# A hybrid attention, RG-LRU and SSD decoder step on one core: loads of rows by store and reload, slots of the background streams, and banks of the output sums

## The chip, the cores and the metric

The kernel runs on one core of one Trainium2 chip. The metric is device time in microseconds of one execution. Engines are named as the profile names them: PE (TensorE matmul), PEld (its weight loads), DVE (VectorE), ACT (ScalarE), POOL (GpSimd) and SP (SyncE, which here only issues DMAs). A "q" behind a name (SPq, ACTq) is that engine's queue of DMA issues.

## The reference, cut to what matters

Two layers work on 1024 prompt tokens and on 8 sample tokens with caches. Each layer is one combined projection, three kinds of heads beside each other, and one output projection.

```python
def mixer_layer(x, pos, att_cache, lru_conv0, lru_h0, ssd_conv0, ssd_h0, p):
    proj = jnp.einsum('bld,de->ble', x, p['w_in'])
    q, k, v, g_att, x_lru, g_lru, z_ssd, xbc, dt_raw = jnp.split(proj, SPLIT_POINTS, axis=-1)
    ...
    br_a = att * jax.nn.silu(g_att)          # 8 query heads, 2 key heads, window 128, sinks
    ...
    br_b = hl * jax.nn.silu(g_lru)           # conv of 4 taps, block gates, linear recurrence
    ...
    y, ssd_h1 = ssd_scan(xh, dt, a_head, ...)  # chunks of 128 tokens, 12 heads of 64, state 128
    y = (y + D * xh) * jax.nn.silu(z_ssd)
    y = y * lax.rsqrt(jnp.mean(jnp.square(y), -1, keepdims=True) + NORM_EPS) * p['ssd_norm_g']
    mix = jnp.concatenate([br_a, br_b, y], -1)
    out = jnp.einsum('ble,ed->bld', mix, p['w_out'])
    return layer_norm(DEEPNORM_ALPHA * x + out, p['ln_g'], p['ln_b']), states
```

In an SSD chunk `a_cs` is a running sum of `dt * a_head` over the 128 tokens. The chunk needs `exp(a_cs[i] - a_cs[j])` for all pairs of tokens, so the kernel needs each head's `a_cs` both as a column and as a row that every partition holds.

## The kernel before, in words

The work is four steps, (layer, half of the tokens), one behind the other: step 0 is layer 0 with tokens 0 to 511, step 1 layer 0 with tokens 512 to 1023 and the 8 sample tokens, steps 2 and 3 the same for layer 1. Half 0 works on 512 columns, half 1 on 520, as two chunks of 260 (`chunks`). By the trace, step 0 ends near 345 us, step 1 near 815, step 2 near 1165 and step 3 at the end.

**The foreground.** `step()` calls the projections in a written order; each makes 128 output channels. A projection is 24 matmuls for 512 columns, or 24 for each of the two chunks, because every product is taken as three (`mac3`, L295 to L297: high part by high part, high by low, low by high). Its sums stand in one of three PSUM banks of the pool `ipp` (`ip_tile()`), and an operation on ACT or DVE empties the bank: `conv` (L328), `gate_silu` (L341 on ACT, L342 on DVE) or `rope`. The fourth part of a step is `out_proj`: four groups of rows (attention, the second part of the SSD rows, LRU, the rest) by eight blocks of 128 outputs, each sum again in an `ip_tile()`, added to the residual by DVE at L1044 (L1053 after the change).

**The background.** Everything else is written as Python generators in lists by name (`att`, `ssd`, `ssd_sub`, `lru`, `norm`, `tail`). Before each 12 matmuls of 512 columns or 24 of 260, `pump()` lets each of them go on by one turn; `yield n` waits n such turns (called slots here), and `spawn(list, generator, delay)` starts one after `delay` slots, 3 if none is given. The sums of the background stand in five banks of the pool `mmp` (`mm_tile()`). `drain` runs lists to their end.

* `attention_stream`: for each of 4 query groups g and 4 blocks of 128 tokens, `block` makes scores (L874, L875), a softmax (L878 to L886), waits 3 slots, transposes the probabilities (L892) and copies them out (L895, L897), waits 2 slots, multiplies by the values (L903) and gates the result into the buffer `ga` (L905). After block 3 the group's `ga` is stored to DRAM (`mixd`, L908, issued by ACT). `ga` has two buffers (`NQ`), so the third group's gate (L342) waits for the first group's store.
* `attention_sample` (half 1): the 8 sample tokens, a chain of small operations with `yield` between the parts. Scores L965 and L966, then on DVE and ACT a softmax that ends with `pr` (L977) and `dg` (L979), `yield 2`, the matmuls L982 and L983, two copies, `yield 2`, the matmuls from L990.
* `ssd_steps`: makes `dt`, `da`, and, in half 1, stores the sample tokens' decays (`sdd`, L539, rows of single numbers) and loads them back spread over the partitions (`dcols`, L542); it stores the 48 transposed running sums (`acsd`, L563).
* `ssd_stream`: for each of 2 head groups and 4 chunks, `block` loads two tiles `acr` of decay rows (L636; 3 heads each, 192 KB, `NA` = 3 buffers) from `acsd`, transposes (L639, L648), builds decays on ACT and POOL (L655 to L662), and 3 slots later multiplies (L667, L672); `weighted` (L607) reads the result. `sample(g)` does the 8 sample tokens: it stores `bcd` (L696), loads it back as `bb` (L705, a pair of tokens at a time), loads each state `h0` (L707) and stores it (L712). `squares` and L755 make the norm's sum.
* `lru_stream`: the block gates L459 want a row move inside a tile by DMA (L430) before their last quarter.

Almost all DMAs are issued by SP, in the order in which they stand. An issue that must wait (for data just stored, or for a buffer) holds all issues behind it, weights among them: `wraw` (L242), and in half 1 `wl` (L244), the low parts of the weights that half 0 computed and stored (`low`). Two projections' weights are loaded ahead (`load_weights`).

The program is built with a scheduler that lays out each engine's instructions by its own estimate of times; the order in which the code emits them is a priority only.

Of the kernel before, what the change touches and what calls it, by code (L numbers as in the profile page):

```python
# [13 lines left out]
AF = mybir.ActivationFunctionType  # L14
# [3 lines left out]
P = 128  # L18
# [23 lines left out]
NA = 3  # L42
# [9 lines left out]
def tile_trunk(ctx, tc, outs, x_t, cache_k, cache_v, st_lru_conv, st_ssd_conv, st_ssd_h, w_in, w_dt, w_out,  # L52
# [6 lines left out]
    dma = nc.sync.dma_start  # L59
# [437 lines left out]
    def ssd_steps(st, l, half, x):  # L497
# [12 lines left out]
        def rest():  # L510
# [21 lines left out]
            if half:  # L532

                sdt = wtile([NS, 2, 12], "eda")
                V.tensor_copy(sdt[:, 0, :], dt[:NS, 48:60])
                S.activation(sdt[:, 1, :], da[:NS, 48:60], AF.Exp)
                sdd = dp.tile([2, 12, NS], F32, tag="sdd", name="sdd")
                for e in range(2):
                    dma(sdd[e].rearrange("k b -> b k"), sdt.rearrange("b q (t e) -> b (q t) e", e=2)[:, :, e])  # L539
                dcols = st["dcols"] = wtile([P, 2, 6, NS], "dcols")  # L540
                for e in range(2):
                    dma(dcols[64 * e:64 * e + 64].rearrange("p a b c -> p (a b c)"),  # L542
                        bview(sdd, e * 96, [[0, 64], [1, 96]]))
            yield 7
# [18 lines left out]
            dma(acsd, acsT)  # L563
            st["steps"] = True
# [32 lines left out]
    def ssd_stream(st, l, half, mixrows):  # L597
# [30 lines left out]
        def block(g, b):  # L628
# [6 lines left out]
            for i in range(2):  # L635
                dma(acr[i], bview(acsd, (eb + 3 * i) * P, [[0, P], [1, 3 * P]]))  # L636
            pt = mm_tile()
# [49 lines left out]
        def sample(g):  # L687
# [9 lines left out]
            yield 1  # L697
# [4 lines left out]
            for b in range(NS):  # L702
                if b % 2 == 0:
                    bb = wtile([P, 2, 2, P], "bb", 2)
                    dma(bb, bview(bcd, b * 2 * P, [[0, P], [1, 4 * P]]))  # L705
                h0, u = wtile([P, 3, P], "h0", 2), wtile([P, 3, P], "sd", ND)
                dma(h0, st_ssd_h[l, b, heads].rearrange("(t e) p n -> (e p) t n", e=2))  # L707
                for t in range(3):
                    S.activation(u[:, t, :], bb[:, b % 2, 0, :], AF.Copy, scale=dcols[:, 0, t, b:b + 1])
# [3 lines left out]
                for t in range(3):  # L713
                    V.tensor_tensor_reduce(u[:, t, :], bb[:, b % 2, 1, :], h0[:, t, :], 1.0, 0.0,  # L714
                                           op0=ALU.mult, op1=ALU.add, accum_out=ysum[:, t, b:b + 1])
# [15 lines left out]
        for g in range(2):  # L731
# [6 lines left out]
            for b in range(4):  # L738
                spawn("ssd_sub", block(g, b))
                yield 4  # L740
# [116 lines left out]
    def attention_stream(st, l, half, mixrows, mixd0):  # L857
        W = HALF + NS * half

        def block(g, b, qa, ga):  # L860
# [26 lines left out]
            yield 3  # L887
# [45 lines left out]
    def attention_sample(l, qs, kn, vT, gas, mixd0):  # L933
# [46 lines left out]
        yield 2  # L980
# [7 lines left out]
        yield 2  # L988
# [19 lines left out]
    def out_proj(l, half, mixd, load_next, first):  # L1008
# [5 lines left out]
        cur = first  # L1014
        for gi, (g, _) in enumerate(GROUPS):
# [16 lines left out]
            for part in ((slice(HALF // 2, W), slice(0, HALF // 2)) if split_c else (None,)):  # L1032
                for op in range(4):
                    w = weights((l, g, op))
                    for oo in range(2):
                        pump()
                        o = 2 * op + oo
                        for cs in ([part] if part else chunks(W)):
                            out = ip_tile()[:, :cs.stop - cs.start]
# [268 lines left out]
```

## Time and profile before

| | |
|---|---|
| time, median of 3 runs (lowest, highest) | 1651.32 us (1650.24, 1659.54) |
| the profiled execution's own time | 1659.71 us |
| its span, first to last instruction | 1658.0 us |
| mean granted clock of TensorE | 0.978 of full speed |
| PE busy | 1573.9 us, 95% |
| DVE, ACT, POOL busy | 1066.0, 965.0, 642.7 us |
| DMA traffic | 337.45 MB, mean 204 GB/s |

Durations and waits below come from that one execution, 8.4 us above the median of the runs. A wait row tells how long an engine stood idle and what ended the idleness. A timeline row has the start in us, the duration in us, engine, line, operation, output <- input, and in brackets the idle time before it with its releaser.

### The profile page before, as it was taken

What the parts mean: (1) busy time and instruction counts of PE and PEld (TensorE: products, weight loads), DVE (VectorE), ACT (ScalarE), POOL (GpSimd) and SP (SyncE); (2) the same over time, 40 slices, a digit from 0 to 9 for tenths busy, and PEclk for the clock granted to TensorE, in tenths of its full rate; (3) what the DMA queues carried; (4) which work ended last, traced back from release to release, by engine and by line L of the source; (5) the groups of instructions that cost most, each with busy time, mean ns of one, the idle gap of its engine ahead of it and who ended that gap; (6) DMA issues with size and microseconds to landing.
All of it is one profiled execution on the core that took longest, in us unless ns stands there. A gap on an engine that the chain in (4) does not pass through costs nothing.

```text
span 1658.0 us, 31019 instructions
## 1 busy us (share of the span) xinstructions
PE 1573.9 (95%) x10696; PEld 1335.0 (81%) x10696; DVE 1066.0 (64%) x2220; ACT 965.0 (58%) x2136; POOL 642.7 (39%) x858
## 2 busy tenths in 40 slices
PE   8999999999989998999998999998999999989996
PEld 6777777678979897889976777775899998978895
DVE  5567659754955756775488675687435568568634
ACT  5565557633656665784256655676346666567724
POOL 5655666553112525200155565765512134341000
PEclk9999999999999998999999999999999999999998
DMA  8654566776554756587546556578865566657865
GB/s 267 192 169 152 164 184 215 270 258 206 170 165 159 235 181 204 179 286 267 186 137 209 181 151 179 153 238 290 244 212 168 171 191 210 199 159 239 303 201 195
DMA packets 210806, 337.45 MB, mean 204 GB/s; under 512 B 24132, under 2 KB 64272, under 8 KB 210600
## 3 DMA queue, kind: packets, MB, share of 16 engines
q1 hardware_dynamic: 208344, 331.27, 62.9%
q10 hardware_dynamic: 2304, 4.20, 0.7%
q8 instruction: 84, 1.38, 0.3%
q14 instruction: 74, 0.61, 0.1%
HBM read 242.76 MB, written 92.05 MB: 202 GB/s over the span
## 4 chain that ended last, share of the span: by engine, by line
PE 62%; DVE 12%; DMA 10%; ACT 6%; issue 3%; POOL 2%; SPq 1%; DVEq 0%; ACTq 0%; POOLq 0%
PE ip L295 17%; PE ip L297 17%; PE ip L296 17%; PE mm L459 2%; PE mm L672 2%; PE mm L903 2%; PE mm L892 2%; DVE u L358 1%; DMA wl<-low 1%; DVE sd L714 1%; DMA out_dram<-h 1%; DMA wraw<-in_w_out_dram 1%; PE mm L667 1%; ACT wh L245 1%; DMA h<-in_st_ssd_h_dram 1%
## 5 line engine op out<-in xcount | busy, mean ns | idle before, releaser
L295 PE MATMUL ip<-u,wh 128*128 128x260 f32 (+3 forms) x2592 | 853.0, 329 | 30.4 <-DVE u L1044 13.0
L297 PE MATMUL ip<-u,wl 128*128 128x260 f32 (+3 forms) x2592 | 839.5, 324 | 8.6 <-DMA wl<-low 7.4
L296 PE MATMUL ip<-u,wh 128*128 128x260 f32 (+3 forms) x2592 | 835.2, 322 | 0.6 <-DVE u L226 0.6
L295 PEld LDWEIGHTS ip<-u,wh 128*128 128x128 f32 x2592 | 494.6, 191 | 93.3 <-issue 22.6
L297 PEld LDWEIGHTS ip<-u,wl 128*128 128x128 f32 x2592 | 493.6, 191 | 56.4 <-DMA wl<-low 9.4
L296 PEld LDWEIGHTS ip<-u,wh 128*128 128x128 f32 x2592 | 494.5, 191 | 38.8 <-issue 2.5
L249 POOL TENSOR_TENSOR wl<-wraw,wh 128x256 fp32r<-128x256 f32 x432 | 369.7, 880 | 253.2 <-ACT wh L247 173.2
L247 ACT ACTIVATE wh<-wraw 128x512 fp32r<-128x512 f32 x216 | 134.3, 625 | 163.7 <-PE ip L296 78.1
L245 ACT ACTIVATE wh<-wraw 128x512 fp32r<-128x512 f32 x224 | 138.8, 625 | 137.3 <-PE ip L296 100.9
L1044 DVE SCALAR_TENSOR_TENSOR u<-u,ip 128x260 f32<-128x260 f32 (+3 forms) x192 | 96.8, 509 | 136.9 <-PE ip L297 132.2
L358 DVE SCALAR_TENSOR_TENSOR u<-ev,ssd_p,u 128x512 f32<-128x512 f32 x120 | 101.1, 843 | 14.6 <-ACT u L350 12.4
L882 ACT ACTIVATE sp<-sp,mx 128x257 f32<-128x257 f32 (+1 forms) x128 | 62.4, 489 | 58.7 <-DVE mx L878 58.7
L656 POOL TENSOR_TENSOR cq<-cq,u 128x384 f32<-128x384 f32 x56 | 61.7, 1104 | 78.6 <-ACT cq L655 55.4
L226 DVE TENSOR_TENSOR u<-u 128x512 fp32r<-128x512 f32 (+1 forms) x88 | 64.7, 763 | 31.2 <-ACT u L225 31.0
L662 ACT ACTIVATE acr<-acr,acs 128x128 f32<-128x128 f32 x192 | 63.4, 390 | 30.9 <-POOL acr L659 30.8
L655 ACT ACTIVATE cq<-acr 128x384 f32<-128x384 f32 x56 | 29.1, 520 | 83.0 <-DMA acr<-acsd 82.1
L358 DVE SCALAR_TENSOR_TENSOR u<-ev,lru_p,u 128x512 f32<-128x512 f32 x72 | 63.6, 886 | 19.9 <-ACT u L350 10.7
L878 DVE CUSTOM_DVE_ANT_0 sp<-mm,amask,sp 128x256 f32<-128x256 f32 (+1 forms) x128 | 54.5, 462 | 33.2 <-PE mm L875 10.4
L342 DVE SCALAR_TENSOR_TENSOR u<-ev,ip 128x260 f32<-128x260 f32 (+1 forms) x72 | 36.4, 507 | 58.4 <-ACT ev L341 58.3
L225 ACT ACTIVATE u<-u 128x512 fp32r<-128x512 f32 (+1 forms) x88 | 52.1, 626 | 31.3 <-DMA u<-mixd 18.1
L328 ACT ACTIVATE ev<-ip 128x260 f32<-128x260 f32 (+2 forms) x132 | 58.2, 442 | 11.6 <-PE ip L297 7.7
L714 DVE CUSTOM_DVE_ANT_0 sd<-bb,h 128x128 f32<-128x128 f32 x96 | 38.0, 443 | 37.8 <-POOL h L711 35.0
(280 smaller groups left out, 2128.0 us busy)
## 6 DMA issues: line engine op xcount, KB each, us to landing
wraw<-in_w_in_dram SPq DMA_DIRECT2D x304, 256.0 KB
wl<-low SPq DMA_DIRECT2D x224, 256.0 KB
low<-wl SPq DMA_DIRECT2D x216, 256.0 KB
wraw<-in_w_out_dram SPq DMA_DIRECT2D x136, 256.0 KB
acr<-acsd SPq DMA_DIRECT2D x64, 192.0 KB
u<-mixd SPq DMA_DIRECT2D x32, 260.0 KB
u<-mixd SPq DMA_DIRECT2D x32, 256.0 KB
mixd<-u SPq DMA_DIRECT2D x24, 260.0 KB
```

The costliest lines, as they stand in the source:

```text
L226: V.tensor_tensor(dl, raw, dh.bitcast(F32), ALU.subtract)
L245: S.activation(h, raw, AF.Copy)
L247: S.activation(h, raw, AF.Copy)
L249: G.tensor_tensor(low[:, c], raw[:, c], h[:, c].bitcast(F32), ALU.subtract)
L295: PE.matmul(out, wh, xh, start=first, stop=False)
L296: PE.matmul(out, wh, xl, start=False, stop=False)
L297: PE.matmul(out, wl, xh, start=False, stop=last)
L358: V.scalar_tensor_tensor(out[:, :HALF], raw[:, t:t + HALF], prm[:, wo + t:wo + t + 1], out[:, :HALF], op0=ALU.mult, op1=ALU.add)
L656: G.tensor_tensor(cq[i], cq[i], zc[:, None, 3, cs].to_broadcast([P, 3, P]), ALU.mult)
L662: S.activation(acr[i][:, e, :], acr[i][:, e, :], AF.Exp, scale=-1.0, bias=nacs[:, eb + 3 * i + e:eb + 3 * i + e + 1])
L882: S.activation(s[:, kv, :nk + 1], s[:, kv, :nk + 1], AF.Exp, scale=-1.0, bias=mx[:, kv:kv + 1], accum_out=den[:, kv:kv + 1])
L1044: V.scalar_tensor_tensor(ro, ro, ALPHA if gi == 0 else 1.0, out, op0=ALU.mult, op1=ALU.add)
```

## The change

Eight edits, none of which changes what is computed:

* `NA`: the `acr` tiles get four buffers for three.
* In `rest()` of `ssd_steps`, the load of `dcols` is written behind the `yield 7`, its store `sdd` ahead of it; and a `yield 3` stands between the store of `acsd` and the mark `steps` that lets the SSD blocks start.
* `block` of the SSD stream waits 3 slots between its two loads of `acr` and its first transposes, and is spawned with a delay of 1 for 3.
* `sample` waits 3 slots for 1 behind its store of `bcd`; `bb` is loaded for each token (128 KB, three buffers) and no longer for each pair (256 KB, two buffers).
* The attention `block` waits 4 slots for 3 ahead of its transposes.
* `attention_sample` waits 5 slots for 2 ahead of `pd` (L982), and 3 for 2 ahead of `po` (L990).
* `out_proj` takes every third sum of the first group, and every second of the others, from the five banks of `mmp` and no longer from the three of `ipp`.

Behind the edits the lines move by 1 to 9: L542 becomes L544, L636 L638, L874 L876, L892 L894, L903 L905, L908 L910, L965 L967, L982 L984, L990 L992.

```diff
--- before.py
+++ after.py
@@ -39,7 +39,7 @@
 NU = 10
 NQ = 2
 ND = 4
-NA = 3
+NA = 4
 NC = 3
 HW = 90
 FX = 1
@@ -537,11 +537,12 @@
                 sdd = dp.tile([2, 12, NS], F32, tag="sdd", name="sdd")
                 for e in range(2):
                     dma(sdd[e].rearrange("k b -> b k"), sdt.rearrange("b q (t e) -> b (q t) e", e=2)[:, :, e])
+            yield 7
+            if half:
                 dcols = st["dcols"] = wtile([P, 2, 6, NS], "dcols")
                 for e in range(2):
                     dma(dcols[64 * e:64 * e + 64].rearrange("p a b c -> p (a b c)"),
                         bview(sdd, e * 96, [[0, 64], [1, 96]]))
-            yield 7
             pc = mm_tile()
             PE.matmul(pc[:, 0:48], tri, da[:, :48], start=True, stop=True)
             PE.matmul(pc[:, 64:112], ones, da[:, :48], start=True, stop=True)
@@ -561,6 +562,7 @@
             V.tensor_copy(acsT, pa[:48, :P])
             acsd = st["acsd"] = dp.tile([48, P], F32, tag="acsd", name="acsd")
             dma(acsd, acsT)
+            yield 3
             st["steps"] = True
 
         spawn("ssd", rest())
@@ -634,6 +636,7 @@
             acr = [wtile([P, 3, P], "acr", NA) for _ in range(2)]
             for i in range(2):
                 dma(acr[i], bview(acsd, (eb + 3 * i) * P, [[0, P], [1, 3 * P]]))
+            yield 3
             pt = mm_tile()
             for i in range(4):
                 PE.transpose(pt[:, i * P:(i + 1) * P], xb[:, i, cs], ident)
@@ -694,24 +697,23 @@
             V.tensor_copy(bcr, pt[:NS, :2 * P])
             bcd = dp.tile([NS, 2 * P], F32, tag="bcd", name="bcd")
             dma(bcd, bcr)
-            yield 1
+            yield 3
             dcols = st["dcols"][:, :, 3 * g:3 * g + 3, :]
             V.tensor_tensor(dcols[:, 0], dcols[:, 0], xb[:, 0:3, cs], ALU.mult)
             ysum = wtile([P, 3, NS], "ysum")
             heads = slice(6 * g, 6 * g + 6)
             for b in range(NS):
-                if b % 2 == 0:
-                    bb = wtile([P, 2, 2, P], "bb", 2)
-                    dma(bb, bview(bcd, b * 2 * P, [[0, P], [1, 4 * P]]))
+                bb = wtile([P, 2, P], "bb", 3)
+                dma(bb, bview(bcd, b * 2 * P, [[0, P], [1, 2 * P]]))
                 h0, u = wtile([P, 3, P], "h0", 2), wtile([P, 3, P], "sd", ND)
                 dma(h0, st_ssd_h[l, b, heads].rearrange("(t e) p n -> (e p) t n", e=2))
                 for t in range(3):
-                    S.activation(u[:, t, :], bb[:, b % 2, 0, :], AF.Copy, scale=dcols[:, 0, t, b:b + 1])
+                    S.activation(u[:, t, :], bb[:, 0, :], AF.Copy, scale=dcols[:, 0, t, b:b + 1])
                 G.tensor_tensor(h0, h0, dcols[:, 1, :, b:b + 1].to_broadcast([P, 3, P]), ALU.mult)
                 G.tensor_tensor(h0, h0, u, ALU.add)
                 dma(s_ssd_h[l, b, heads].rearrange("(t e) p n -> (e p) t n", e=2), h0)
                 for t in range(3):
-                    V.tensor_tensor_reduce(u[:, t, :], bb[:, b % 2, 1, :], h0[:, t, :], 1.0, 0.0,
+                    V.tensor_tensor_reduce(u[:, t, :], bb[:, 1, :], h0[:, t, :], 1.0, 0.0,
                                            op0=ALU.mult, op1=ALU.add, accum_out=ysum[:, t, b:b + 1])
                 yield 1
             while ("ssd", g, 7) not in st:
@@ -736,7 +738,7 @@
             if half:
                 spawn("ssd_sub", sample(g))
             for b in range(4):
-                spawn("ssd_sub", block(g, b))
+                spawn("ssd_sub", block(g, b), 1)
                 yield 4
             if half:
                 spawn("tail", final_state(g))
@@ -884,7 +886,7 @@
             V.reciprocal(den, den)
             V.tensor_scalar(s[:, 0, :nk], s[:, 0, :nk], den[:, 0:1], None, op0=ALU.mult)
             S.activation(s[:, 1, :nk], s[:, 1, :nk], AF.Copy, scale=den[:, 1:2])
-            yield 3
+            yield 4
             pp = mm_tile()
             for kv in range(2):
                 for kh in range(nkh):
@@ -977,7 +979,7 @@
         V.tensor_scalar(pr, pr, m[:, 1:2], None, op0=ALU.mult)
         dg = wtile([64, 64], "dg")
         V.tensor_scalar(dg, ident[:64, :64], pr[:, P:P + 1], None, op0=ALU.mult)
-        yield 2
+        yield 5
         pd = mm_tile()
         PE.matmul(pd[:NS, :64], bsel, dg, start=True, stop=True)
         PE.transpose(pd[:, 64:128], pr[:, :P], ident[:64, :64])
@@ -985,7 +987,7 @@
         V.tensor_copy(d8, pd[:NS, :64])
         pTs = wtile([P, 64], "pTs")
         V.tensor_copy(pTs, pd[:, 64:128])
-        yield 2
+        yield 3
         po = mm_tile()
         PE.matmul(po[:, :64], kvn[:, 1, :], d8, start=True, stop=False)
         for b in range(NS):
@@ -1012,6 +1014,13 @@
         for i in range(2):
             dma(r[i][:, :, :W], xd[l, half][512 * i:512 * i + 512, :W].rearrange("(k p) w -> p k w", p=P))
         cur = first
+        outs = [0]
+
+        def out_tile(gi):
+
+            outs[0] += 1
+            return mm_tile() if outs[0] % (3, 2)[gi > 0] == 0 else ip_tile()
+
         for gi, (g, _) in enumerate(GROUPS):
             if gi == 1 and half == 0:
 
@@ -1036,7 +1045,7 @@
                         pump()
                         o = 2 * op + oo
                         for cs in ([part] if part else chunks(W)):
-                            out = ip_tile()[:, :cs.stop - cs.start]
+                            out = out_tile(gi)[:, :cs.stop - cs.start]
                             for k in range(4):
                                 mac3(out, w.part(k, slice(oo * P, oo * P + P)), mh[:, k, cs], ml[:, k, cs],
                                      k == 0, k == 3)
```

The places where the order of the program shows what moved, row by row as it stands on an engine:

On SP in step 3, where the sample tokens' decays are stored and loaded back (`wl` and `wraw` are weights, `eda` holds the decays). Before:

```order
L244 DMA wl_14408<-low_176 128x512
L242 DMA wraw_14576<-in_w_in_dram 128x512
L539 DMA sdd_14232<-eda_14229 8x12x1 x2
L542 DMA dcols_14235<-sdd_14232 64x96 x2
L244 DMA wl_14478<-low_177 128x512
L242 DMA wraw_14582<-in_w_in_dram 128x512
```

and after:

```order
L244 DMA wl_14421<-low_176 128x512
L242 DMA wraw_14592<-in_w_in_dram 128x512
L539 DMA sdd_14248<-eda_14245 8x12x1 x2
L544 DMA dcols_14528<-sdd_14248 64x96 x2
L244 DMA wl_14491<-low_177 128x512
L242 DMA wraw_14598<-in_w_in_dram 128x512
```

The load of `dcols` stands directly behind the store in both, though the code now has seven slots between them; in step 1 two row moves of the rope (L779, L780) stand between the two, before and after alike.

On PE in step 1, the sample tokens' attention from its scores (`sT`, `prod`) to the use of `dg`. A line of "..." stands for the rest of the SSD block's part (L672, L648) and 24 matmuls of the projections (L295 to L297), the one ahead of L982 for 44 of these. Before:

```order
L965 MATMUL mm_7623<-ident_77,sT_7413 64x128
L966 MATMUL mm_7623<-ones_83,prod_6858 64x1
L667 MATMUL mm_7654<-sd_7447,q_7449 128x384
...
L639 MATMUL mm_7717<-ident_77,u_6208 128x128 x4
...
L982 MATMUL mm_7794<-dg_7637,bsel_85 8x64
L983 MATMUL mm_7794<-ident_77,spr_7630 128x64
```

and after, where each "..." holds the rest of the part ahead of it (L675, L651, a second L459 row) and 24 matmuls of the projections:

```order
L967 MATMUL mm_7613<-ident_77,sT_7377 64x128
L968 MATMUL mm_7613<-ones_83,prod_6866 64x1
...
L670 MATMUL mm_7683<-sd_7493,q_7495 128x384
...
L642 MATMUL mm_7761<-ident_77,u_6149 128x128 x4
...
L459 MATMUL mm_7837<-u_7210,gw_88 32x260 x4
...
L459 MATMUL mm_7900<-u_7210,gw_88 32x260 x4
...
L984 MATMUL mm_7952<-dg_7627,bsel_85 8x64
```

Between the scores and the matmul that reads `dg` stood an SSD block's products, 24 matmuls of a projection, the next block's transposes and 44 matmuls more; now five times 24 matmuls, the SSD products, an SSD block's transposes and two pairs of gates stand there.

On PE in step 1, in the attention blocks (`sp` is the buffer of scores and of transposed probabilities). Before, with 24 projection matmuls at the "...":

```order
L903 MATMUL mm_5904<-sp_5768,vtok_93 64x128 x4
L892 MATMUL mm_5910<-ident_77,sp_5701 128x128 x4
...
L874 MATMUL mm_5982<-kh0_89,qa_5327 128x256
L875 MATMUL mm_5982<-kl0_91,qa_5327 128x256
L874 MATMUL mm_5982<-kh1_90,qa_5328 128x256
L875 MATMUL mm_5982<-kl1_92,qa_5328 128x256
L903 MATMUL mm_6039<-sp_5915,vtok_93 64x128 x4
```

and after, the same place with nothing left out:

```order
L905 MATMUL mm_5929<-sp_5801,vtok_93 64x128 x4
L894 MATMUL mm_5935<-ident_77,sp_5701 128x128 x4
L876 MATMUL mm_5954<-kh0_89,qa_5327 128x256
L877 MATMUL mm_5954<-kl0_91,qa_5327 128x256
L876 MATMUL mm_5954<-kh1_90,qa_5328 128x256
L877 MATMUL mm_5954<-kl1_92,qa_5328 128x256
L905 MATMUL mm_6056<-sp_5940,vtok_93 64x128 x4
L894 MATMUL mm_6062<-ident_77,sp_5805 128x128 x4
```

L892 fills the bank from which the probabilities `sp_5915` are copied, and 24 matmuls and the four scores stood between it and L903, which reads them. Now only the four scores of the next block stand between L894 and the L905 that reads `sp_5940`.

## Rows read from the trace of the kernel before

**Rows 1.** The page, engines: busy time, share of the span, instructions

```profile
PE 1573.9 (95%) x10696; PEld 1335.0 (81%) x10696; DVE 1066.0 (64%) x2220; ACT 965.0 (58%) x2136; POOL 642.7 (39%) x858
```

**Rows 2.** The page, chain that ended last, by engine

```profile
PE 62%; DVE 12%; DMA 10%; ACT 6%; issue 3%; POOL 2%; SPq 1%; DVEq 0%; ACTq 0%; POOLq 0%
```

**Rows 3.** Waits of PE: line <- releaser: total us, times, longest

```profile
PE ip L295 <- DVE u L1044: 13.0, 11, 3.7
PE ip L297 <- DMA wl<-low: 7.4, 8, 3.8
PE ip L295 <- DVE ga L342: 7.2, 2, 5.7
PE mm L982 <- DVE dg L979: 7.0, 1, 7.0
PE mm L982 <- ACT ev L341: 6.2, 1, 6.2
PE mm L903 <- DVE sd L607: 5.6, 2, 3.0
PE mm L903 <- ACT sp L897: 3.2, 3, 2.3
```

**Rows 4.** PE by stretch: from:to, length, busy (matmuls), granted clock, DMA share, GB/s

```profile
337.74:344.56 6.82, 6.11 (x14) 0.50 0.97 293
651.76:662.00 10.24, 6.14 (x34) 0.50 0.48 150
662.00:672.24 10.24, 10.24 (x100) 1.00 0.52 144
1156.94:1163.76 6.82, 5.81 (x14) 0.50 0.89 275
1467.55:1474.37 6.82, 4.74 (x28) 0.50 0.58 180
```

**Rows 5.** PE's two lines around the sample tokens' softmax, first and last start

```profile
L966 PE MATMUL mm<-ones,prod x4: 197/207/218, 636.2 to 1450.3; 128*64 128x1 f32 x4
L982 PE MATMUL mm<-dg,bsel x4: 259/285/311, 655.9 to 1469.7; 64*8 64x64 f32 x4
```

**Rows 6.** DVE timeline in the output projection of step 0

```profile
334.22 1.23 DVE L226 TENSOR_TENSOR u<-u 128x512 fp32r<-128x512 f32 x1
335.37 1.21 DVE L476 SCALAR_TENSOR_TENSOR hb<-hb 128x512 f32<-128x512 f32 x1
336.50 1.21 DVE L226 TENSOR_TENSOR u<-u 128x512 fp32r<-128x512 f32 x1
337.63 0.68 DVE L1044 SCALAR_TENSOR_TENSOR u<-u,ip 128x512 f32<-128x512 f32 x1
```

**Rows 7.** Waits of SP's queue: total us, times, longest

```profile
SPq L707 <- DMA out_dram<-h: 51.2, 24, 4.6
SPq L542 <- DMA sdd<-eda: 14.4, 2, 8.2
SPq L636 <- DMA acsd<-q: 8.2, 4, 3.8
```

**Rows 8.** Waits of ACT and DVE: total us, times, longest

```profile
ACT cq L655 <- DMA acr<-acsd: 82.1, 29, 6.2
DVE ga L342 <- DMA mixd<-ga: 11.9, 5, 4.8
```

**Rows 9.** PE timeline in the attention blocks of step 1

```profile
514.10 0.66 PE L892 MATMUL mm<-ident,sp 128*128 128x128 f32 x4
517.47 0.28 PE L874 MATMUL mm<-kh,qa 128*128 128x256 f32 x1
521.78 0.66 PE L903 MATMUL mm<-sp,vtok 128*64 128x128 f32 x8
```

**Rows 10.** PE timeline, the LRU's gates at the end of step 1

```profile
710.15 2.39 PE L459 MATMUL mm<-u,gw 96*32 96x260 f32 x30
718.44 1.50 PE L459 MATMUL mm<-u,gw 96*32 96x260 f32 x6
```

## The prediction, made before the changed kernel had run

> **What bounds the kernel now.** I read the page's engine line first: PE is busy 1573.9 of 1658.0 us, DVE, the next, 1066.0 [rows 1]. The chain of waits that ended last says the same with more detail: 62% of it is PE, 12% DVE, 10% DMA [rows 2]. So PE is the bound, the change takes no matmul away, and all that can be won is in the 84 us (1658.0 - 1573.9) in which PE stands still, plus what the clock costs after a standstill. The waits of PE say who ended these idle times [rows 3]: DVE's additions in the output projection (L1044, 13.0 us), the sample tokens' `dg` (two waits on L982, 7.0 and 6.2 us; the second is put down to ACT, but by the order L982 reads what DVE writes at L979), the low weights (7.4), the gate `ga` (7.2), and L607's release of a buffer (5.6).
>
> A standstill costs more than its length. By stretches, PE's granted clock was 0.50, its lower level of 1.2 GHz, from 651.76 to 662.00, after and during the wait for `dg`, and 34 matmuls stand there; in the 10.24 us behind it, at 1.00, there are 100 [rows 4]. So I price a wait as its length plus half of PE's busy time in the stretch at 0.50 around it.
>
> **The change, part by part.**
>
> *Sample tokens' slots (`yield` 2 to 5 ahead of L982).* Step 1: 6.2 + 6.14 / 2 = 9.3 us; step 3: 7.0 + 4.74 / 2 = 9.4 [rows 3, 4]. Together 18.7. From the scores' last matmul to L982 19.7 us pass (655.9 - 636.2) and 19.4 in step 3 (1469.7 - 1450.3) [rows 5]; less the waits, PE had 13.5 and 12.4 us of work there. Where 24 + 44 projection matmuls stood, the order now has 5 times 24, 52 more, and two pairs of gates (32 matmuls) besides; the SSD block's parts stay. At 0.10 us each (10.24 us for 100 [rows 4]) the 52 are 5.3 us, the gates, of which 30 took 2.39 us [rows 10], 2.5: 7.8 us of further work, 0.8 to 1.6 more than the waits. DVE's chain to `dg` must not grow by more than that, and among it stand the states' operations, which move as well; so I take 16 of 18.7. Bounds: 9 (the softmax on DVE comes later by what it gained, and half is left) to 18.7.
>
> *Sums from two pools (L1044).* The long waits are 3.7 us each, in steps 0 and 2. DVE's timeline shows why: two operations of the next group's split (L226) and one of the LRU (L476), 1.2 us each, stand between a finished sum and its addition at 337.63 [rows 6]. PE has three banks; with a third of the first group's sums elsewhere, and half of the later ones', it can go one or two sums further (a sum has 12 matmuls of 512 columns; 14 of them took 6.11 us at half the clock [rows 4], so some 2.6 us) before it needs that bank. Price of the two: 3.7 + 6.11 / 2 = 6.8, and 3.7 + 5.81 / 2 = 6.6, and 13.0 - 7.4 = 5.6 in nine short ones [rows 3, 4]: 19.0 at most. I take 13, as the long ones shrink to under 1 us; nothing is the other end, if DVE's additions stay in the order and PE catches up with them a sum later.
>
> *`acr` rows ahead (four buffers, three slots).* ACT waits 82.1 us in 29 times for these rows [rows 8], yet PE has no long wait that names them. What reaches PE is L607, two waits of 5.6 us in all, in steps 1 and 3 [rows 3]; DVE stands behind ACT's late decays there. With half the same clock price behind each it is some 9 us. The loads are hidden now, but SP, too, is held by the states' stores, 51.2 us, 24 times [rows 7], and that is not touched. I take 3; bounds 0 and 9.
>
> *`dcols` later.* SP waited 14.4 us in two times for the store `sdd` (L542) [rows 7]; behind it stand the weights, and the low weights are 7.4 us of PE's waits [rows 3]. But the order shows that the scheduler issues the load directly behind the store as before. I take 0. Two long waits of PE hang on it and stay: 5.7 us in step 1 in the row of `ga`, where DVE, ahead of its gate, stands behind a row move of the rope that SP issues after `dcols`, and in step 3 the longest of the low weights', taken as half of that row, 3.7 [rows 3]. With half of such a stretch at 0.50 behind each (6.14 / 2 to 4.74 / 2 [rows 4]) they are some 14 us together. Bounds 2 us either way.
>
> *`bb` for each token.* 32 loads of 128 KB for 16 of 256 KB. In the states' loop SP stands 51.2 us behind stores [rows 7], and the added issues lie in that time. If they did not, they would hold up weights; the nearest row is that of the low weights, about 1 us a wait (7.4 in eight [rows 3]), one in each of steps 1 and 3. I take 0, bounds -2 (a first token's rows are there sooner) and +2.
>
> *What becomes tighter.* (a) The attention block's fourth slot: in step 1, L903 came 7.0 us after the end of the transposes whose copy it reads (521.78 - 514.10 - 0.66 [rows 9]); at one place in each of steps 1 and 3 only four scores of the next block stand between them now, some 0.6 us of PE, and the copy by ACT must fit into that. The nearest rows are the three waits on that copy (L897), 3.2 us, longest 2.3 [rows 3]: 0 to 2.3 each, I take 2 in all. (b) The stores of `ga` come up to a slot later, and the gate waits for them: 11.9 us in five times on DVE [rows 8]; what PE sees beyond today's is 0 to 8, I take 3. (c) The LRU's last quarter of gates now stands directly behind the first three quarters, where 8.3 us lay between the starts (718.44 - 710.15) [rows 10]; the row move that it needs is issued between them behind the SSD rows' stores. 1 to 4 us in each of steps 1 and 3; I take 3 in all. (d) SSD blocks come a slot later, and with them the sum for the norm (L755): 0 to 2 each in steps 0 and 2; I take 2. Sum of the losses 10, bounds 2 to 25 (4.6 + 8 + 8 + 4).
>
> **Sum.** 16 + 13 + 3 - 10 = 22 us less. The profiled execution took 1659.71 us and would take 1637.7; it lies 8.4 us above the median of 1651.32, and none of the terms is in that difference, so the median would go to about 1630. By the bounds: the best is 18.7 + 19 + 9 - 2 = 45 less, the worst of the same mechanisms 25 - 9 = 16 more.
>
> **Rivals.**
>
> *No gain in the output projection.* The sums' additions are DVE's, and the next group's splits stay in its way; DMA's share was 0.97 in that stretch [rows 4], so the next wait may be for weights. Then 13 goes, 9 us less are left: 1642. The Trainium skill, in "TensorE: Matmul & The Clock Gate", section "HAM oscillation", reports a kernel to which a second PSUM buffer brought no further gain after its loop had been put in another order. By it the time would be this rival's. For it speaks that nine of the eleven waits are short ones, which a further bank may only move; against it, that PE's rows name the bank's release, and that the addition at 337.63 is late by a burst of 3.6 us [rows 6], not much more than the one sum that a further bank covers. So it has less than the forecast.
>
> *The tighter places win.* One mechanism: the gate's buffer `ga`. There are two buffers for four groups, and each store now comes a slot (24 matmuls of 260 columns, about the same; 2.8 us taken) later, while the gate that needs the buffer stays where it is among the projections. Today DVE stands 4.8 us at most [rows 8] and PE sees 1.5 of it (7.2 in two waits, one of 5.7 [rows 3]); a slot more makes 4.3 us of PE, with a clock stretch of 6.82 us behind it, 3.4: 7.7 a time. At two reuses in each of four steps that is 62 us, and 7 for the other losses, against 32 won: 37 more, 1688. It decides from the point where more than three of the eight reuses wait so long (25 / 7.7). Against it: in steps 0 and 2 a projection's matmuls are longer, and only five waits were seen in eight.
>
> *The decays' load moves after all.* If the queue, unlike the order, lets the weights through, because the store is issued earlier, the two waits with their clock, 14 us, go as well: 1616. For it speaks nothing in the order.
>
> **How the numbers follow.** Forecast as above 0.5; no gain from the sums 0.25; the tighter places 0.13 (half of it fully, the rest between 1650 and 1688); the decays' load, or the best of the bounds, 0.12. The range has to take in the first two and part of the outer ones: 1608 to 1660. The forecast's own range is 1618 to 1640. A measurement of this kernel tells apart about 1%, 16.5 us. Faster than 1634.8: most of the forecast's 0.5 (0.38) and all of the last case, 0.12, is 0.5. Slower than 1667.8: 0.1. The rest, 0.4, is within.
>
> **What would show it.** Right: L984 on PE waits under 1 us in both steps and the clock stays at 1.00 there; the waits on DVE's additions fall from 13.0 to under 4; ACT's waits for `acr` fall from 82.1 to under 20; L544 on SP still waits 12 to 16 for `sdd`, with PE's two long waits behind it still there. Losses: waits of PE on L905 by ACT's copy, on L459 behind the row move, and on `ga`, of 1 to 3 us each. Wrong: a new wait of over 3 us in steps 1 or 3 with the clock at 0.50 behind it, or the output projection waiting for weights as long as it did for DVE.

## The result, and the profile after

| | before | after |
|---|---|---|
| median of 4 runs (lowest, highest), us | 1650.78 (1648.97, 1659.54) | 1665.87 (1663.11, 1668.63) |
| the profiled execution, its span, us | 1659.71, 1658.0 | 1668.63, 1666.9 |
| PE busy, us | 1573.9 | 1572.5 |
| granted clock, mean | 0.978 | 0.975 |

The ratio is 1.0081, 95% interval 1.0052 to 1.0111: 15 us slower by the medians, 8.9 by the spans of the two profiled executions. 1630 had been forecast, and the range ended at 1660. The rows below can account only for the 8.9, since the profiled execution of before was the slowest of its four. PE's work is the same, so the loss is again in waits.

The steps tell where. Each is taken here to the end of its last addition in the output projection; by this the steps before the change end at 397.9, 826.0 and 1217.2 us, not near the 345, 815 and 1165 that were named ahead of the prediction. From:to, length, PE busy (matmuls), granted clock, DMA share, GB/s; before, and after:

```profile
0.00:397.90 397.90, 379.63 (x1899) 0.98 0.66 209
397.90:826.00 428.10, 405.79 (x3416) 0.98 0.64 203
826.00:1217.20 391.20, 378.22 (x1906) 0.98 0.64 200
1217.20:1658.00 440.80, 410.26 (x3481) 0.97 0.63 202
```

```profile
0.00:390.80 390.80, 376.82 (x1899) 1.00 0.66 213
390.80:831.80 441.00, 409.43 (x3416) 0.95 0.62 197
831.80:1218.20 386.40, 376.30 (x1906) 1.00 0.62 203
1218.20:1666.90 448.70, 409.93 (x3481) 0.96 0.62 199
```

Steps 0 and 2 are 7.1 and 4.8 us shorter, steps 1 and 3 are 12.9 and 7.9 longer: the change wins in half 0 and loses in half 1.

PE's waits after the change (line, releaser, total us, times, longest), the answer to [rows 3]:

```profile
PE mm L387 <- POOL last_h L482: 12.3, 2, 6.2
PE mm L459 <- DMA u<-u: 10.6, 2, 5.6
PE mm L459 <- DMA mixd<-u: 9.9, 1, 9.9
PE mm L459 <- issue: 9.8, 1, 9.8
PE ip L295 <- ACT wh L247: 9.8, 4, 6.8
PE mm L905 <- ACT sp L899: 5.6, 4, 2.3
PE ip L295 <- DVE ga L342: 5.0, 1, 5.0
PE mm L894 <- DVE sp L887: 4.7, 1, 4.7
PE ip L297 <- DMA wl<-low: 4.1, 3, 3.2
PE mm L297 <- POOL wl L249: 3.1, 2, 1.6
PE ip L297 <- POOL wl L249: 2.8, 9, 0.7
```

Everything that the change was forecast to remove is gone: no row for the sums (13.0 in [rows 3]), for `dg` (13.2) or for L607 (5.6; L609 after the change). In its place stand 30.3 us on the LRU's gates L459 (10.6 + 9.9 + 9.8) and 12.3 on L387, the transpose of the LRU's last states; neither had a row before. 31.8 us went and 42.6 came.

ACT's and DVE's waits (answer to [rows 8]) and SP's for `sdd` (to [rows 7]):

```profile
ACT cq L658 <- PE mm L675: 23.1, 15, 2.9
DVE ga L342 <- DMA mixd<-ga: 8.0, 5, 3.0
ACT cq L658 <- DMA acr<-acsd: 7.4, 6, 2.3
```

```profile
SPq L544 <- DMA sdd<-eda: 12.2, 2, 6.5
```

The loads ahead work: ACT's 82.1 us of waits for `acr` are 7.4. They were not what PE waited for. The store of `sdd` holds SP as before (12.2 for 14.4).

PE by stretches, with the granted clock, around one of the two longest new waits (9.84 us, ended at 710.93), one on L387 (6.22, ended at 766.18) and one on the first gates L459 (5.04, ended at 644.84):

```profile
704.80:715.00 10.20, 4.07 (x10) 0.50 0.78 264
715.00:725.30 10.30, 10.30 (x75) 0.83 0.66 232
762.90:769.70 6.80, 3.52 (x17) 0.50 0.33 108
643.40:650.20 6.80, 5.36 (x26) 0.50 0.76 233
```

The clock is at its lower level, 0.50, in the stretches in which these waits end, and at 0.83 in the mean of the stretch behind the longest: by the prediction's price 9.8 + 4.07 / 2 is 11.9, without what the second stretch still lost.

### The profile page after: what moved, and what is told of

It is laid out like the page before. It is cut to its first block, busy times and chain, and to the rows that moved or that the text cites. A ratio compares the mean times of both kernels' runs of the same rounds, so it can differ in the third digit from the quotient of the medians.

```text
span 1666.9 us, 30981 instructions
## 1 busy us (share of the span) xinstructions
PE 1572.5 (94%) x10696; PEld 1334.2 (80%) x10696; DVE 1055.8 (63%) x2220; ACT 980.0 (59%) x2144; POOL 641.0 (38%) x858
## 5 line engine op out<-in xcount | busy, mean ns | idle before, releaser
L295 PE MATMUL ip<-u,wh 128*128 128x260 f32 (+2 forms) x2248 | 737.7, 328 | 15.5 <-ACT wh L247 9.8
L297 PE MATMUL ip<-u,wl 128*128 128x260 f32 (+2 forms) x2248 | 728.5, 324 | 7.4 <-DMA wl<-low 4.1
L296 PE MATMUL ip<-u,wh 128*128 128x260 f32 (+2 forms) x2248 | 725.2, 323 | 0.0
L295 PEld LDWEIGHTS ip<-u,wh 128*128 128x128 f32 x2248 | 430.0, 191 | 70.7 <-ACT wh L247 15.2
L249 POOL TENSOR_TENSOR wl<-wraw,wh 128x256 fp32r<-128x256 f32 x432 | 376.1, 895 | 274.9 <-ACT wh L247 197.1
L297 PEld LDWEIGHTS ip<-u,wl 128*128 128x128 f32 x2248 | 429.3, 191 | 51.5 <-POOL wl L249 11.4
L296 PEld LDWEIGHTS ip<-u,wh 128*128 128x128 f32 x2248 | 429.3, 191 | 30.6 <-issue 0.3
L297 PE MATMUL mm<-u,wl 128*128 128x260 f32 (+3 forms) x344 | 111.9, 325 | 3.1 <-POOL wl L249 3.1
L295 PE MATMUL mm<-u,wh 128*128 128x260 f32 (+3 forms) x344 | 112.1, 326 | 0.0
L296 PE MATMUL mm<-u,wh 128*128 128x260 f32 (+3 forms) x344 | 111.2, 323 | 0.0
L358 DVE SCALAR_TENSOR_TENSOR u<-ev,ssd_p,u 128x512 f32<-128x512 f32 x120 | 97.8, 815 | 18.3 <-ACT u L350 10.2
L1053 DVE SCALAR_TENSOR_TENSOR u<-u,ip 128x260 f32<-128x260 f32 (+3 forms) x106 | 53.9, 509 | 63.2 <-PE ip L297 62.5
L459 PE MATMUL mm<-u,gw 96*32 96x260 f32 (+1 forms) x576 | 63.5, 475 | 30.4 <-DMA u<-u 10.6
L1053 DVE SCALAR_TENSOR_TENSOR u<-u,mm 128x260 f32<-128x260 f32 (+3 forms) x86 | 43.6, 507 | 63.3 <-PE mm L297 63.1
L358 DVE SCALAR_TENSOR_TENSOR u<-ev,lru_p,u 128x512 f32<-128x512 f32 x72 | 59.5, 829 | 27.4 <-ACT u L350 26.7
L342 DVE SCALAR_TENSOR_TENSOR u<-ev,ip 128x260 f32<-128x260 f32 (+1 forms) x72 | 36.0, 507 | 63.0 <-ACT ev L341 59.8
```

Source lines behind the costliest of these rows:

```text
L249: G.tensor_tensor(low[:, c], raw[:, c], h[:, c].bitcast(F32), ALU.subtract)
L295: PE.matmul(out, wh, xh, start=first, stop=False)
L296: PE.matmul(out, wh, xl, start=False, stop=False)
L297: PE.matmul(out, wl, xh, start=False, stop=last)
L358: V.scalar_tensor_tensor(out[:, :HALF], raw[:, t:t + HALF], prm[:, wo + t:wo + t + 1], out[:, :HALF], op0=ALU.mult, op1=ALU.add)
L459: PE.matmul(ps[c0:c1, :n], gw[:, gi, k, b0:b0 + c1 - c0], xc[:96, k, cs], start=True, stop=True, skip_group_check=True)
```

## The experiments

Three causes were on trial, the third in three wordings. A: sums that take background banks keep the LRU's gates waiting for banks, so that its chain ends later. B: the wait on `dg` had covered the LRU's first row move. C, later D and E: the edits of the rows, and of these the SSD block's one later slot, bring the SSD's chain and the row moves behind it too late for PE. Each ratio is to the kernel before, run on the same chip, with its 95% interval.

### One part alone: e1 to e3

e1 has only the edit of `out_proj`, e2 only the two yields of `attention_sample` (2 to 5, 2 to 3), e3 only the edits of NA, `rest`, `block` and `sample`. e1:

```diff
-                            out = ip_tile()[:, :cs.stop - cs.start]
+                            out = out_tile(gi)[:, :cs.stop - cs.start]
```

> The kernel before with the one edit of out_proj (sums from both pools). Theory A: the five background banks, now shared with the sums, give the LRU's gates their banks later, so the last gates stand only 48 projection matmuls ahead of the transpose of last_h (L387), which then waits for POOL's copy: two waits of about 6 us with half clock behind, some 16 us, as in the changed kernel. Against it stands the end of L1044's waits (13.0 us and clock, 19 us). Together 1646 to 1650 us. Rival: L387's wait comes from the rows' slots, not from the banks: no wait on L387, and 1632 us.

Measured 0.9988 (0.9967 to 1.0010). PE's waits of e1:

```profile
PE mm L387 <- POOL last_h L482: 11.3, 2, 5.6
PE ip L295 <- DVE ga L342: 7.7, 3, 5.4
PE mm L982 <- DVE dg L979: 7.5, 1, 7.5
```

A holds: L387's wait comes with the banks alone. The order on PE says how. With five banks for the background, the third pair of the second set of gates was done after 96 projection matmuls, and 84 stood between the last gate and L387; with the sums in the same banks that pair is done only after 168, and only 48 are left between the last gates and L387.

> The kernel before with only the sample tokens' slots (2 to 5 and 2 to 3). Theory B: the wait on dg (13.2 us, 18.7 with the clock) had covered the LRU's first row move (L430), which SP issues behind the states' stores; without it the first gates L459 wait for it, about 5 us and clock in steps 1 and 3, 15 us: 1645 to 1650 us. The last quarter of the later gates has 72 projection matmuls ahead of it and waits under 2 us. Rival: the row move is late because of the rows' edits; then L459 doesn't wait here, and the time is 1632 us.

Measured 0.9989 (0.9963 to 1.0016): no wait on `dg`, and this row instead:

```profile
PE mm L459 <- DMA u<-u: 11.2, 3, 6.9
```

B holds. The gates stand where they stood; PE comes to them some 6 us earlier and meets the row move.

> The kernel before with the edits of the rows alone (four acr buffers, slots behind the stores, blocks' spawn, bb for each token). Theory C: these alone put the last quarter of the LRU's gates directly behind the first three quarters, and PE waits there for the row move L430, near 10 us with clock, in steps 1 and 3, some 24 us; the waits on L607 (5.6 us, 9 with clock) go; dg's waits stay: 1663 to 1668 us, the whole loss of the changed kernel. Rival: the last quarter waits because PE came earlier (banks, sample slots); then the wait here is under 4 us and the time 1642 to 1650.

Measured 1.0111 (1.0085 to 1.0137): the loss is here. But the wait on the last quarter was 7.9 us in two, not near 20, so C had its place right and its size wrong: with `dg`'s wait still there PE comes later. Another wait was larger, for a bank that L609 releases, twice what it was on L607 (5.6):

```profile
PE mm L642 <- DVE sd L609: 12.1, 2, 6.3
PE mm L984 <- DVE dg L981: 8.4, 1, 8.4
PE mm L459 <- DMA wraw<-in_w_out_dram: 7.9, 2, 4.1
```

### The change less one part: e4 and e5

e4 takes every sum from the three banks again.

> The changed kernel with all sums from the three banks again. Theory A: L387's two waits (12.3 us, some 16 with clock) go and L1053's come back in part (up to 19 us): 1660 to 1670 us, no more than 0.4% from the changed kernel. The two waits of the last quarter on L459 stay at 9 to 10 us (theory C). Rival: the banks are the net loss: 1650 us or less.

Measured 1.0069 (1.0046 to 1.0092), against 1.0081 with the banks: what they give they take. The last quarter's two waits on L459 were 9.6 and 9.3 us.

e5 leaves out the SSD block's edit:

```diff
-            yield 3
             pt = mm_tile()
...
-                spawn("ssd_sub", block(g, b), 1)
+                spawn("ssd_sub", block(g, b))
```

> The changed kernel with the SSD block as before (no yield behind its acr loads, spawned with delay 3). Theory D: of the rows' edits it is this one that makes the SSD's last stores late against PE and so puts the last quarter of the LRU's gates directly behind the first three; without it the order has 72 projection matmuls between them, and the two waits of 9.8 and 9.9 us (24 with clock) go, while the waits on the first row move (10.6) and on L387 (12.3) stay: 1637 to 1645 us. Rival: the loss is spread over the rows' edits (bb by token, the slots behind acsd and bcd): 1655 or more.

Measured 1.0021 (1.0003 to 1.0038), and the waits on the last quarter are gone but for 1.4 us. Of 1.0081, 0.6% is this edit. The time won is less than the 1637 to 1645 us (0.992 to 0.997) that had been expected: a wait for the bank that L609 releases, which the changed kernel does not have, is here with 10.1 us in two.

### The block's slots alone, and where the row move waits: e6 and e7

> The kernel before with only the SSD block's two slots edits (yield 3 behind its loads, spawn with delay 1). Theory D: all of the loss of the rows' edits: ratio 1.008 to 1.013, with a wait of some 4 us on the last quarter of the gates L459 in steps 1 and 3 and one of some 6 us on L609's release ahead of the SSD's transposes. Rival: within 0.3% of the kernel before, and the loss is made by the loads for each token.

Measured 1.0173 (1.0140 to 1.0206): alone it costs more than all the rows' edits together, against 1.008 to 1.013 expected. L459's two waits were 8.2 us, L607's 10.0, and the low weights' 11.9. With three `acr` buffers ACT still waits 77.6 us for the rows (82.1 before), so this run has the late slot without loads ahead that work.

e7 issues the row moves elsewhere:

```diff
-                dma(xc[32 * i:32 * i + 32, 3, :W], xc[96:P, i, :W])
+                (G.dma_start if half else dma)(xc[32 * i:32 * i + 32, 3, :W], xc[96:P, i, :W])
```

> The changed kernel with the LRU's row moves (L430) of half 1 issued by POOL's queue and no longer by SP's. If these gates wait because the row move stands in SP's queue behind the states' and the SSD rows' stores, all four waits on L459 (5.0, 9.8, 5.6, 9.9 us; 39 with clock) shrink to under 3 us each: 1635 us or less. Rival: the data itself is late (the convolution on DVE), or POOL's own queue holds it: the waits stay within 2 us of what they were, 1660 or more.

Measured 1.0077 (1.0053 to 1.0101):

```profile
PE mm L459 <- DMA u<-u: 25.4, 4, 7.5
```

The four waits are 25.4 us in all, from 30.3: the rival, in the main. What happens is in the changed kernel's own rows around 700 us. PE, which has done three quarters of four gate tiles by 701.1:

```profile
699.14 1.96 PE L459 MATMUL mm<-u,gw 96*32 96x260 f32 x24
710.93 1.48 PE L459 MATMUL mm<-u,gw 96*32 96x260 f32 x3 [9.84 <-issue]
```

DVE, on which the last tap of the convolution (L358) stands behind the SSD norm's reciprocal and its six products:

```profile
692.93 3.39 DVE L759 RECIPROCAL ssq<-ssq 128x520 f32<-128x520 f32 x1
...
699.24 4.11 DVE L763 SCALAR_TENSOR_TENSOR u<-u,lru_p,ssq 128x520 f32<-128x520 f32 x6
703.27 0.74 DVE L358 SCALAR_TENSOR_TENSOR u<-ev,lru_p,u 128x512 f32<-128x512 f32 x1
```

and SP, on which the row move stands behind the stores of these six products:

```profile
704.39 2.94 SPq L765 DMA_DIRECT2D mixd<-u  x4
707.41 0.67 SPq L430 DMA_DIRECT2D u<-u  x1
```

The tap ends at 704.0, 2.9 us after PE is ready. SP adds 3.4 until it issues the move (707.41), and the move takes 3.5 until PE goes on (710.93). On POOL's queue the wait at this place was 7.2: the queue is some 2.6 of the 9.8, the rest is DVE's lateness against PE and the move itself. In the kernel before, the order had 48 projection matmuls between the three quarters and the last [rows 10]; after the change it has none.

### The late slot itself: e9, and cover in its place: e10

```diff
-            yield 3
+            yield 2
             pt = mm_tile()
```

A block spawned with delay 1 starts at the next slot; with `yield 3` it computes in the fourth, and a block spawned with delay 3 in the third. `yield 2` keeps the loads ahead and gives the old slot back.

> The changed kernel with yield 2 for 3 behind the SSD block's acr loads: loads still ahead, but the block computes in the slot in which it did before (spawned with delay 1 it starts one slot later than delay 3 less 2). Theory E: it is the one slot by which the SSD's chain comes later that costs, not the loads ahead; the order has 72 projection matmuls ahead of the last quarter of the gates again, and its waits (19.7 us) fall under 3: 1638 to 1650 us. Rival: the loads ahead hold SP and so the weights; then 1660 or more.

Measured 1.0009 (0.9989 to 1.0028), the waits of the last quarter gone:

```profile
PE mm L387 <- POOL last_h L482: 12.8, 2, 6.5
PE mm L459 <- DMA u<-u: 9.0, 2, 5.7
PE mm L642 <- DVE sd L609: 8.5, 2, 4.4
```

E holds for the cause: one slot is worth 0.7%, 12 us, and loading ahead is not at fault. It is less than the 1638 to 1650 us that had been expected (0.992 to 0.9995), and the 8.5 us on L609's release, which came back as in e5, are a part of the difference. The same place in e9 shows that cover decides, and not the time at which DVE is done:

```profile
701.60 1.95 PE L459 MATMUL mm<-u,gw 96*32 96x260 f32 x24
705.18 0.75 DVE L358 SCALAR_TENSOR_TENSOR u<-ev,lru_p,u 128x512 f32<-128x512 f32 x1
706.76 0.54 SPq L430 DMA_DIRECT2D u<-u  x1
```

The tap ends at 705.9, later than the changed kernel's 704.0, and the move is issued 0.7 us earlier than there. But 72 projection matmuls stand behind the three quarters, PE comes to the last quarter only at 712.55, and it doesn't wait.

e10 keeps the late slot and puts the second set of gates two slots later:

> The changed kernel with only the second set of the LRU's gates two slots later in half 1 (yield 5 for 3). If PE stands at the last quarter because DVE's last convolution tap (L358) comes behind the SSD norm's six products (L763), two slots of cover end it: L459's waits of 9.8 and 9.9 us go (24 with clock): 1640 to 1648 us. L387 waits as long as before or up to 6 us longer, since its chain begins later (then up to 1655). Rival: something else is late by as much in this place and the time stays within 4 us of the changed kernel.

Measured 1.0162 (1.0132 to 1.0192), outside both expectations: worse than the changed kernel. No gate waits at that place, but

```profile
PE ip L295 <- DVE u L342: 20.0, 2, 10.2
```

PE now runs into the projections' own banks, which DVE empties: L342 stands on DVE behind the same products and the splits after them. DVE alone is not the reason, though. It has done what stands ahead of L342 at 706.87 and then idles:

```profile
708.18 1.10 DVE L342 SCALAR_TENSOR_TENSOR u<-ev,ip 128x260 f32<-128x260 f32 x3 [1.32 <-issue]
```

By the semaphore that L342 waits for, it is released by one of the products' stores (L765), landed at 708.1. Moving the gates gave no cover: PE meets the products' chain, on DVE and in their stores, with whatever stands there.

### What is left when the costly parts go: e8, e11 to e14

e8 is the kernel before with the sample tokens' slots and the shared banks, the first gates two slots later in half 1, and L387's stream spawned with delay 8.

> The kernel before with the two edits that pay (sample tokens' slots, sums from both pools) and with a cure for what each uncovered: the LRU's first gates two slots later in half 1 (yield 5 for 3), and the transpose of last_h spawned with delay 8 for 3. By theories A and B the waits on dg (18.7 with clock) and L1044 (19) go and no wait on L459 or L387 comes: 1615 to 1625 us, ratio 0.98 to 0.985. Rival: PE meets another late chain as soon as these go, and the time stays within 0.5% of before.

Measured 0.9969 (0.9942 to 0.9996), as the rival says: L387 still waited 3.6 and 3.9 us, and instead of the gates L342's bank held PE for 4.9 and 3.8. e11 leaves the gates alone and, in half 1, keeps the sums out of the banks until the last group:

```diff
-            return mm_tile() if outs[0] % (3, 2)[gi > 0] == 0 else ip_tile()
+            return mm_tile() if outs[0] % (3, 2)[gi > 0] == 0 and (half == 0 or gi == 3) else ip_tile()
```

> The kernel before with the sample tokens' slots and with the sums from both pools only where the LRU's gates don't run beside them (all of half 0, the last group of half 1). By theory A L387 doesn't wait and the two long waits on L1044 go (13.4); by theory B dg's waits go (18.7) and some 15 come back on the first gates L459: 1630 to 1640 us. Rival: as with the two edits alone, each gain is given back to the next late chain: within 0.3% of before.

Measured 0.9931 (0.9906 to 0.9955), 1645.45 us beside 1656.91 on that chip:

```profile
PE mm L459 <- DMA u<-u: 10.9, 3, 5.3
PE ip L295 <- DVE u L1051: 4.1, 5, 1.4
PE mm L387 <- POOL last_h L482: 0.8, 1, 0.8
```

The expectation had said that no gates run beside the sums in half 0. They do: in step 0 the first sum in a background bank is added at 305.7 and the last gates run to 321.9. But the transpose L387 stands in half 1 only. And by the profile the win is the banks' in half 0: steps 0 and 2 take 391.7 and 384.1 us (397.9 and 391.2 before), steps 1 and 3 are within 0.6 of before. The sample tokens' slots give back on the first gates (10.9) what they take from `dg` (13.2), as in e2; the banks of half 0 without these slots were not run. On another chip:

> The sample tokens' slots and the two pools in half 0 and the last group, again, for an interval on another chip: ratio to the kernel before 0.990 to 0.996. Rival: the first measurement was the chip's, and the interval holds 1.

0.9949 (0.9925 to 0.9973): it is some 0.5% faster than the kernel before, and so faster than the changed one.

e12 is e13 (below) with the first gates two slots later:

> All edits of the change, but with the SSD block in its old slot (yield 2), the two pools for the sums only in half 0 and the last group, and the LRU's first gates two slots later in half 1. By theories A, B and E no wait on L459's last quarter, on L387, on dg or long ones on the sums, and L609's waits shortened: 1615 to 1630 us. Rival: DVE's and POOL's chains in steps 1 and 3 are as long as PE's work there; then other waits take the place and the time is 1640 or more.

Measured 0.9988 (0.9966 to 1.0010): the rival; L342's bank (15.0 us in five) took the place, as in e8 and e10, and L609's release holds PE for 12.7 (8.2 in e13). e13 has every edit of the change with `yield 2` and with e11's banks.

> All edits of the change, with the SSD block in its old slot (yield 2) and the two pools for the sums only in half 0 and the last group. If the block's slot and the shared banks beside the LRU's gates are the two parts that made the change slower, nothing is left that does: the last quarter of the gates waits under 2 us, L387 doesn't wait, and the time is 1640 to 1648 us, as with the two paying edits alone. Rival: the acr loads ahead themselves cost (L642 behind L609's release, 4.1 and 4.4 us with the old slot), and the time is 1652 to 1660.

Measured 0.9940 (0.9915 to 0.9964). So all edits but these two make the kernel 0.6% faster, and with the block's late slot and the banks shared beside the gates of half 1 it is 0.8% slower: some 1.4% of the time, 23 us, is theirs. The rest of the edits (loads ahead, `dcols`, `bb` for each token, the attention's slot) add nothing that can be seen beside e11 and e14 (0.9931, 0.9949); none of them was run alone.

## Why the prediction was wrong, point by point

**Right.** The waits on the sums and on `dg` went entirely, as forecast (13 + 16 us). `acr`: 82.1 to 7.4, under 20 as said. The decays' load: its order was the same, SP waited 12.2, and PE's wait that hangs on `ga` stayed, at 5.0 for 5.7; the last low-weight wait of 3.2 stayed too. The copy of the probabilities: four waits of 5.6 us for three of 3.2, 2.4 more where 2 were taken.

**Right by luck.** L607's two waits went too, of which a third (3 us) was counted, but not because ACT has its rows in time. In e9 and e13 the loads are ahead (ACT waits 14.4 and 12.4 us for `acr`, for 82.1), and PE still waits 8.5 and 8.2 us on L609's release, more than the 5.6 before. What holds DVE up ahead of L609 is not ACT but the sample tokens' states; e9:

```profile
541.31 0.83 POOL L712 TENSOR_TENSOR h<-h,dcols 128x384 f32<-128x384 f32 x1 [6.13 <-DMA h<-in_st_ssd_h_dram]
543.26 0.29 DVE L716 CUSTOM_DVE_ANT_0 sd<-bb,h 128x128 f32<-128x128 f32 x1 [4.32 <-POOL h L713]
547.52 0.85 DVE L609 SCALAR_TENSOR_TENSOR sd<-u,dcol,mm 128x128 f32<-128x128 f32 x3
```

POOL waits for the load of a state, DVE for POOL, and PE, at L642 (548.52), for DVE. In the kernel before DVE idles 4.8 and 4.2 us for POOL at the same operation (L714) ahead of L607. The wait is gone only where the late slot and the sample tokens' slots come together; why it is gone there stays open.

**Term (c), the gates' last quarter.** This is the step of the prediction that failed, beside two waits that it did not have at all (the first gates and L387, below). Forecast 3 us in all, at most 8; measured 9.8 + 9.9, with the clock some 24. It named the place and the queue, and with `dg`'s waits still there its bound of 4 us a step about holds: 4.1 and 3.8 in e3. But it was worked out as if the other terms left PE where it was; it did not ask when DVE would have the data and when PE, with `dg`'s wait gone, would come. The row move's source stands on DVE behind 7.5 us of the SSD norm (3.39 + 4.11), and nothing on PE covers it.

**Term (d), the SSD's later slot.** Forecast 0 to 2 us each in steps 0 and 2. These steps became shorter; in steps 1 and 3, which the term left out, the slot decides the last quarter's cover: e9 takes the slot back and 0.7% comes with it.

**The sample tokens' slots.** The gain was counted at 16 us and what is late next was asked of DVE's chain to `dg` only. The first gates, which stand next to L982 on PE, were late as well: e2 wins `dg`'s waits (13.2), gives 11.2 us to L459, and has the time of before (0.9989). In the changed kernel the first gates wait 10.6 us, which stood in no term.

**The sums' banks.** Banks of the background were counted as free. They were the LRU's gates' (e1): L387's two waits, 12.3 us, stood in no term and in no rival.

**What the sum lacked.** By the prediction's own price (the wait and half of PE's busy time in the stretch at 0.50) the last quarter is 21 us more than counted, L387 12.3 + 3.5 = 16 and the first gates 10.6 + 5.4 = 16: 53 us, an estimate. Against them the removed waits were worth up to 15 more than the 32 counted (18.7 + 19 + 9), and `ga`'s 3 did not come. That leaves 35, and 1630 was missed by 36; so close an agreement is partly chance, as the profiles lie up to 9 us from the medians.

**The rivals.** The slower case was given to `ga`; its waits on DVE fell instead, from 11.9 to 8.0. The case without a gain from the sums did not come about as it was argued: their waits went, and no longer waits for weights took their place (the low weights 4.1 us for 7.4). What the Trainium skill reports in "TensorE: Matmul & The Clock Gate", section "HAM oscillation", no further gain from a second PSUM buffer, agrees with the time of e1 (0.9988), where L387's waits took what the banks gave. It does not agree with e11: there the banks are shared in half 0 and the last group, the waits on the sums fall to 4.1 us, and the ratio is 0.9931, where the sample tokens' slots alone have 0.9989.

## What to carry to other kernels

When a wait of PE is taken away, PE arrives earlier at everything behind it: list what it reaches in the next ten microseconds, and when each operand is ready on the engine and the queue that make it, before the wait is counted as won. A bank or a slot taken from a background stream has a price where that stream's chain ends, which may be a hundred microseconds further on. And a delay that is written as "load now, compute three slots later" has to be counted from the stream's old start: here it was one slot too many, and giving it back was worth 12 us.

## What the runs showed of the hardware that was not expected

A reciprocal of 128x520 f32 on DVE took 3.39 us, as long as five of the scalar-tensor-tensor operations of that width (0.69 each). A row move inside a tile (32 rows of 520 numbers) took 3.5 us from its issue on SP until the matmul that waited for it began, and on POOL's queue the profile of e7 has 1.9 to 4.6 us to landing for the twelve moves of half 1, 3.7 in the median. What stays open: why the scheduler's order has cover ahead of the last quarter with the old slot and none with the new one.
